# Attention stage: the first turn of the softmax weights put behind the score burst, the next tile's cast two steps later, the rotations of the opening at two places per chunk

## The chip, the cores and the metric

The kernel runs on one core of a Trainium2 chip. A core has TensorE (PE in the profile), VectorE (DVE), ScalarE (ACT), GpSimd (POOL) and SyncE (SP), each with an instruction queue of its own that is worked off in order; they meet at semaphores. DMAs are issued from the queues of SP (q1 in the profile) and ACT (q10) here. The metric is the device time of one execution in microseconds; of several executions the median counts.

## What is computed

One step of a two-layer hybrid encoder for 2048 prompt tokens and 32 sample tokens, 1024 wide. The first layer is a gated delta rule and is not touched. The second is sliding-window attention: 16 query heads of 64 elements in groups of four on 4 key heads, chunks of 64 tokens, each of which sees its own chunk and the two before it, with a learned sink in the softmax.

```
def sink_softmax(s, sinks):
    m = jnp.maximum(s.max(-1, keepdims=True), sk)
    p = jnp.exp(s - m)
    return p / (p.sum(-1, keepdims=True) + jnp.exp(sk - m))
...
def swa_layer(x, k, v, pos, cached, w_in, sinks, w_out, ln_g, ln_b):
    proj = x @ w_in
    q = rope_partial(proj[..., :B_QW].reshape(b, l, B_Q_HEADS, B_HD), pos) * (B_HD ** -0.5)
    z = proj[..., B_QW:]
    o = cached_attention(q, k, v, sk) if cached else banded_attention(q, k, v, sk)
    out = (o * jax.nn.silu(z)) @ w_out
    return layer_norm(DN_ALPHA * x + out, ln_g, ln_b)
```

## The kernel before

The program is a row of stages that are tied together by hand. Inside `with tc.manual_schedule(engines={PE, DVE, Activation})` the order of the instructions on these three engines is the order in which the Python generators emit them; the order on POOL and SP is chosen by the framework, which may put a load ahead of its place in the program. The stage that is changed is the last one: attention and output projection, from 1758 us to the end at 2180 us of the profiled execution.

Ahead of it P2 makes the projections of the second layer. Its last products (query heads for the first 416 tokens, three units of `plain`, 24 half-products of six matmuls of 128x416) are left over and are laid between the first chunks of the attention. Each half-product is one step of the generator `late`; every second step also issues a weight load on ACT's queue (L1308), and every fourth copies the finished sum from PSUM to a tile `a` on ACT (L1373) and notes down a rotation for later. `after()` takes up to two such notes: a rotation is a shuffle, two products with sin and cos and, at the following call, an addition, all on DVE (L1465 to L1472), and a store on SP (L1473). In the kernel before, `plain` calls `after()` at each step with a full product.

**One chunk** of the attention, number n, with m the one before it:

- `scores(n)`: 16 matmuls into the PSUM tile pair S (L1597), then on DVE for both halves p = 0, 1 the row maximum (L1603), the minimum with the sink (L1604) and their difference (L1605).
- `exps(n, p)`: four exponentials with row sums on ACT (L1615) and one for the sink (L1617).
- `norm(n, p)`: on DVE one over the sum (L1623, L1624), on POOL the scaling of the weights P (L1627).
- `turn(m, p)`: six transposes on PE (L1670), three into each of two PSUM tiles `tr`; the first three are copied to SBUF by ACT, the other three by DVE (both L1672). There are two `tr` buffers in all, one while the opening runs, so each of these bursts waits for the copies of the one before it.
- `values(m)`: 16 matmuls (L1695, L1700), then the product with the gate z into `graw` on DVE (L1706).

Two chunks make a tile of 128 tokens for the output projection. `ready()` takes a finished tile: it loads the residual `r` (L1784), casts `graw` to `g_hi` on ACT (L1787) and makes the remainder `g_lo` on POOL (L1788). `finish()` multiplies the tile with the output weights, 48 matmuls into `po` in eight steps of six (j = 0 to 7, lines L1818 to L1820), adds the residual (L1823) and takes the statistics of the layer norm. The norm itself is put off to step j = 2 of the following tile: an activation on ACT (L1834), a product and a sum on POOL (L1835, L1836), and the store. `outs()` strings the tiles together and calls `ready()` for the next one at the first step with j >= 4 at which one is finished.

**Order of one chunk in the loop** (`beside(n)`, 28 chunks with scores and one without):

```
scores(n); exps(n, 0); step; turn(m, 0); exps(n, 1); norm(n, 0); step; turn(m, 1); norm(n, 1); step; step; values(m)
```

A tile has eight steps and a chunk takes four, so chunks alternate: in the first of a pair (called A in what follows) the steps j = 0 to 3 run, in the second (B) j = 4 to 7, with the cast of the next tile at j = 4.

`opening()` does the same for the chunks 10 to 13 with a half-product of `late` at each `yield`; `first()` handles chunk 14, with the first four steps of the output projection.

Of the kernel before, what the change touches and what calls it, by code (L numbers as in the profile page):

```python
# [10 lines left out]
F32 = mybir.dt.float32  # L11
# [8 lines left out]
D = 1024  # L20
# [1114 lines left out]
class P2:  # L1135
# [10 lines left out]
    def __init__(self, tc, ring, right, mid, I, O, T, G):  # L1146
        self.tc, self.nc, self.I, self.O, self.T, self.G = tc, tc.nc, I, O, T, G
        self.wp = new_pool(tc, ring, "p2_w", self.RING, side="right")
        self.kp = new_pool(tc, ring, "p2_keep", 1, side="right")
        nsk = self.kp.tile([128, 8], F32, tag="nsk", name="nsk")  # L1150
        sks = self.kp.tile([128, 4], F32, tag="sks", name="sks")
        for i in range(2):
            self.nc.sync.dma_start(nsk[i * 64:i * 64 + 64, :], I["sinks"][i].partition_broadcast(64))
        for i in range(4):
            self.nc.sync.dma_start(sks[i * 32:i * 32 + 32, :], I["sinks_s"][i].partition_broadcast(32))
        for t in (nsk, sks):
            self.nc.gpsimd.tensor_scalar(out=t[:], in0=t[:], scalar1=-1.0, scalar2=None, op0=ALU.mult)
# [8 lines left out]
        self.fine = False  # L1166
        self.turn = 0
        self.todo, self.second, self.staged = [], [], []

# [170 lines left out]
        for u in units:  # L1340
            yield from (self.plain if u[2] == 0 else self.winograd)(u)

    def after(self):

        second, self.second = self.second, []
        for f in second:
            f()
        for _ in range(2):
            if self.todo:
                then = self.todo.pop(0)()  # L1350
                if then is not None:
                    self.second.append(then)

    def rest(self):
        while self.todo or self.second:
            self.after()

    def plain(self, unit):
        kind, j, _ = unit
        nc = self.nc  # L1360
        x = list(zip(*self.x0))
        for c in range(2):
            ps = (self.ppl or self.ppr).tile([128, 512], F32, tag="ps", name="ps")[:, :TB]
            for h in range(2):
                w = self.weight(unit, self.PLAIN[c][h])
                for ks in ((0, 1), (2, 3)) if self.fine else (range(4),):
                    if ks[0] == 2:
                        yield 1.13
                    self.product(ps, w, x[4 * h:4 * h + 4], h == 0, h == 1, ks)
                self.load()  # L1370
                if h == 1:
                    a = self.wk.tile([128, TB], F32, tag="ra", name="a", bufs=4)
                    nc.scalar.activation(a[:], ps, AF.Copy, scale=self.SCALES[kind])  # L1373
# [107 lines left out]
class Attention:  # L1481
# [23 lines left out]
    def open_right(self, right, pieces):  # L1505
        nc, tc = self.nc, self.tc
        R = "right"
        self.otwo = new_pool(tc, right, "u_two", 2, side=R)
        self.oone = new_pool(tc, right, "u_one", 1, side=R)
# [65 lines left out]
        return c0 * 64, nk, pair, at, one, 0 if one is None else (one - c0) * 64  # L1575

    def scores(self, n):
        nc, V, thr = self.nc, self.nc.vector, self.thr
        qs = self.start(n)[0]
        tiles = []  # L1580
        for p in range(2):
# [7 lines left out]
            else:  # L1589
# [7 lines left out]
                        nc.tensor.matmul(S[:, half, u, :nk], qs[hs, n % 2, p * 4 + 2 * u:p * 4 + 2 * u + 2, :],  # L1597
                                         kT[hs, p, k0:k0 + nk], start=True, stop=True)
                tiles.append((S[:, :, :, :nk].rearrange("r h u k -> r (h u) k"), self.nsk[:, p * 4:p * 4 + 4]))
        for p, (S, sink) in enumerate(tiles):  # L1600
            c = S.shape[1]
            nm, es_ = (thr.tile([128, 4], F32, tag=t, name=t, bufs=4) for t in ("nm", "es"))
            V.tensor_reduce(out=nm[:, :c], in_=S, axis=AX.X, op=ALU.max, negate=True)  # L1603
            V.tensor_tensor(out=nm[:, :c], in0=nm[:, :c], in1=sink, op=ALU.min)  # L1604
            V.tensor_tensor(out=es_[:, :c], in0=nm[:, :c], in1=sink, op=ALU.subtract)  # L1605
            self.probs[n, p] = S, nm, es_

    def exps(self, n, p):
        nc, thr = self.nc, self.thr
# [99 lines left out]
        elif n % 2 == 1:  # L1709
            self.pend.append(((n - 1) * 64, 128, graw))  # L1710

    def opening(self, chunks):

        yield
        yield
        for n in chunks:
            self.scores(n)
            self.exps(n, 0)
            if self.prev is None:
                self.exps(n, 1)  # L1720
                for _ in range(5):
                    yield
                self.norm(n, 0)
                self.norm(n, 1)
                yield
            else:
                for i, step in enumerate(itertools.chain(self.turn(self.prev, 0), self.turn(self.prev, 1))):
                    if i == 1:
                        self.exps(n, 1)
                    yield  # L1730
                    if i >= 2:
                        self.norm(n, i - 2)
                yield
                self.values(self.prev)
            self.prev = n
        yield

    def first(self, n):

        m, self.prev = self.prev, n  # L1740
        got = self.ready()
        self.out = self.outs(got)
        self.scores(n)
        self.exps(n, 0)
        drain(self.turn(m, 0))
        self.exps(n, 1)
        self.norm(n, 0)
        drain(self.turn(m, 1))
        self.norm(n, 1)
        for _ in range(4):  # L1750
            next(self.out)
        self.values(m)

    def beside(self, n):

        m, self.prev = self.prev, n
        if n is not None:
            self.scores(n)
            self.exps(n, 0)
        next(self.out)  # L1760
        drain(self.turn(m, 0))
        if n is not None:
            self.exps(n, 1)
            self.norm(n, 0)
        next(self.out)
        drain(self.turn(m, 1))
        if n is not None:
            self.norm(n, 1)
        next(self.out)
        next(self.out)  # L1770
        self.values(m)

    def rest(self):
# [6 lines left out]
    def ready(self):  # L1780
        nc, pool = self.nc, self.otwo
        t0, n, graw = self.pend.pop(0)
        r = pool.tile([128, D], F32, tag="r", name="r")
        nc.sync.dma_start(r[:n], self.T["h"][t0:t0 + n, :])  # L1784
        ghi = pool.tile([128, KC, 128], F32R, tag="g_hi", name="g_hi")
        glo = pool.tile([128, KC, 128], F32R, tag="g_lo", name="g_lo")
        nc.scalar.copy(ghi[:, :, :n], graw[:, :, :n])  # L1787
        nc.gpsimd.tensor_tensor(out=glo[:, :, :n], in0=graw[:, :, :n], in1=ghi[:, :, :n], op=ALU.subtract)  # L1788
        return t0, n, r, ghi, glo

    def outs(self, got):

        while got is not None:
            ahead = None
            last = self.late and not self.pend
            for j in self.finish(*got, last):
                if j == 2:
                    for f in self.todo:
                        f()
                    self.todo = []  # L1800
                if j >= 4 and ahead is None and self.pend:
                    ahead = self.ready()
                yield
            got = ahead
# [69 lines left out]
def program(tc, I, O, T, G):  # L1874
# [79 lines left out]
    with tc.manual_schedule(engines={ET.PE, ET.DVE, ET.Activation, ET.Pool}):  # L1954
# [7 lines left out]
        p2.first_keys()  # L1962
        drain(itertools.islice(late, 35))
        p2.rest()
    p2.ppl = None
    left.close()
    mid.close()
    att = Attention(tc, left, p2.keep, I, O, T, G)
    order = list(range(10, 32)) + ["s"] + list(range(10))
    p2.fine = True  # L1970
    with tc.manual_schedule(engines={ET.PE, ET.DVE, ET.Activation}):
        att.load_k(8, 14)
        att.load_v(8, 14)
        loads = iter(((14, 18), (18, 24), (24, 32)))
        for i, _ in enumerate(att.opening([order.pop(0) for _ in range(4)])):
            drain(itertools.islice(late, 1))
            if i in (8, 13, 18):
# [4 lines left out]
        p2.rest()  # L1982
        right.close()
        att.open_right(right, p2.out)
        att.first(order.pop(0))
# [147 lines left out]
```

## Time and profile before

| | us |
|---|---|
| time, median of 3 runs (2180.78 to 2184.08) | 2183.53 |
| the profiled execution's own time | 2181.37 |
| its span | 2179.6 |
| start of the scores of chunk 10 (attention begins) | 1757.97 |
| start of the scores of chunk 11, 12, 13 | 1766.58, 1787.52, 1799.69 |
| start of the scores of chunk 14 (`first`) | 1813.18 |
| start of the scores of chunk 15 (loop begins) | 1832.20 |
| end of the loop's last chunk with scores | 2137.85 |

The page gives PE 95% of the span busy, and the stretches of the table are what matters here: the opening with `first` takes 74 us, the loop 306 us, and 42 us follow. A row of the timeline gives start, duration, engine, line, operation, what it writes and reads, and in square brackets how long its engine had been idle before it and what ended that. Matmuls are pipelined, so their durations overlap; the distance between starts is the time that one costs. Rows marked ACTq or SPq are DMA issues on those queues. A row of the groups gives count, busy time and mean duration in ns, then the idle time before them and who ended it.

### The profile page before, as it was taken

Reading aid. Unit: us, or ns where it says so; the run is one execution under the profiler, and the core shown is the slowest. Engines: PE = TensorE matmul, PEld = TensorE weight load, DVE = VectorE, ACT = ScalarE, POOL = GpSimd, SP = SyncE. Lnnn points to the kernel's source line nnn. Section 1 sums busy time; section 2 is a strip of 40 time slices with the busy share of each in tenths; the row PEclk is TensorE's granted clock in tenths of the full one; section 3 lists DMA queues with packets and bytes.
Section 4 is the critical chain, followed back from the end, with each engine's and each line's share of the span. In section 5 each row is a group of like instructions: output and inputs, shape, how many; then the busy total and the mean of one; then the engine's idle time right before and its main releaser. Section 6 shows DMA issues by size and latency. Waiting matters only on the chain. (4 is left out here: it accounts for less than half of the span.)

```text
span 2179.6 us, 37384 instructions
## 1 busy us (share of the span) xinstructions
PE 2068.7 (95%) x13494; PEld 1874.1 (86%) x13494; DVE 1477.4 (68%) x2767; ACT 906.8 (42%) x2405; POOL 725.1 (33%) x1194
## 2 busy tenths in 40 slices
PE   8999999999989999999789999999999988999998
PEld 6999999999989889888778887899999976777666
DVE  5788977886557588888875665555645655666663
ACT  5545545444422476767662111411221033444441
POOL 1212211151111187878861220000000053666565
PEclk9999999999999999999999999999999999999999
DMA  7755655557764644534845675988888885433321
GB/s 283 226 187 192 214 180 185 188 180 244 257 211 157 209 128 153 163 130 152 274 144 148 209 264 192 340 290 278 291 279 282 283 291 168 110 85 93 99 81 58
DMA packets 342410, 430.28 MB, mean 197 GB/s; under 512 B 69952, under 2 KB 269984, under 8 KB 342208
## 3 DMA queue, kind: packets, MB, share of 16 engines
q1 hardware_dynamic: 304016, 304.78, 44.0%
q10 hardware_dynamic: 38208, 123.10, 16.9%
q8 instruction: 107, 1.75, 0.3%
q14 instruction: 79, 0.65, 0.1%
HBM read 269.72 MB, written 158.44 MB: 196 GB/s over the span
## 5 line engine op out<-in xcount | busy, mean ns | idle before, releaser
L77 PE MATMUL ps<-act_hi,w_hi 128*128 128x416 f32 x1280 | 458.6, 358 | 5.7 <-DVE z L322 2.5
L79 PE MATMUL ps<-act_hi,w_lo 128*128 128x416 f32 x1280 | 450.5, 353 | 4.7 <-POOL w_lo L54 3.3
L78 PE MATMUL ps<-act_lo,w_hi 128*128 128x416 f32 x1280 | 451.1, 352 | 0.0
L77 PEld LDWEIGHTS ps<-act_hi,w_hi 128*128 128x128 f32 x1280 | 242.0, 189 | 10.1 <-DVE z L322 4.3
L79 PEld LDWEIGHTS ps<-act_hi,w_lo 128*128 128x128 f32 x1280 | 241.9, 189 | 9.5 <-POOL w_lo L54 4.4
L78 PEld LDWEIGHTS ps<-act_lo,w_hi 128*128 128x128 f32 x1280 | 242.6, 190 | 2.8
L1330 PE MATMUL ps<-xs_h,w 128*128 128x416 f32 x560 | 199.6, 356 | 7.8 <-DVE ra L1391 6.6
L1331 PE MATMUL ps<-xs_l,w 128*128 128x416 f32 x560 | 199.9, 357 | 0.5 <-DVE xs_l L1228 0.5
L54 POOL TENSOR_TENSOR w_lo<-w_raw,w_hi 128x1024 fp32r<-128x1024 f32 x32 | 81.5, 2547 | 355.2 <-ACT w_hi L53 341.2
L1332 PE MATMUL ps<-xs_h,w 128*128 128x416 f32 x560 | 198.6, 355 | 0.0
L295 DVE SCALAR_TENSOR_TENSOR y<-R,convw,y 128x2083 f32<-128x2083 f32 (+2 forms) x78 | 175.1, 2245 | 24.5 <-ACT y L293 24.3
L1615 ACT ACTIVATE P<-S,nm 128x192 f32<-128x192 f32 (+2 forms) x260 | 105.3, 428 | 177.4 <-DVE nm L1604 170.8
L585 POOL TENSOR_TENSOR tm<-L,Tt 128x60 f32<-128x60 f32 (+19 forms) x375 | 136.3, 363 | 94.2 <-PE sp L760 48.9
L588 POOL TENSOR_TENSOR Tt<-Tt,tm 128x60 f32<-128x60 f32 (+19 forms) x375 | 142.0, 379 | 28.3
L1530 POOL MEMSET vd<- 64x768 f32 (+2 forms) x10 | 7.8, 776 | 398.1 <-DVE ra L1391 397.8
L1627 POOL TENSOR_TENSOR P<-P,sm 128x512 f32<-128x512 f32 (+2 forms) x126 | 101.7, 831 | 87.8 <-DVE sm L1624 69.2
L1330 PEld LDWEIGHTS ps<-xs_h,w 128*128 128x128 f32 x560 | 106.5, 190 | 10.6 <-DVE ra L1391 7.3
L1391 DVE SCALAR_TENSOR_TENSOR ra<-ps,u 128x416 f32<-128x416 f32 x60 | 35.4, 590 | 117.3 <-PE ps L1332 110.7
L1052 PE MATMUL po<-wo,g_hi 128*128 128x512 f32 (+1 forms) x272 | 110.0, 404 | 0.9 <-DVE hT L1100 0.9
L1332 PEld LDWEIGHTS ps<-xs_h,w 128*128 128x128 f32 x560 | 107.1, 191 | 1.3
L1331 PEld LDWEIGHTS ps<-xs_l,w 128*128 128x128 f32 x560 | 106.3, 190 | 2.1 <-DVE xs_l L1228 0.7
L95 ACT CAST pre_hl<-pre_raw 128x256 fp32r<-128x256 f32 x184 | 65.6, 404 | 101.4 <-DMA pre_raw<-in_b_w_z 25.8
(313 smaller groups left out, 4723.6 us busy)
## 6 DMA issues: line engine op xcount, KB each, us to landing
w<-s_w ACTq DMA_DIRECT2D x180, 512.0 KB, 4.5
s_w<-pre_hl SPq DMA_DIRECT2D x160, 256.0 KB, 2.5
w_raw<-in_w_in SPq DMA_DIRECT2D x32, 512.0 KB, 6.6
s_wo<-pre_hl SPq DMA_DIRECT2D x64, 256.0 KB, 4.1
gb<-s_gcum SPq DMA_DIRECT2D x34, 256.0 KB, 5.2
k<-s_k SPq DMA_DIRECT2D x34, 256.0 KB, 3.8
s_z<-z SPq DMA_DIRECT2D x40, 208.0 KB, 2.0
s_q<-y SPq DMA_DIRECT2D x8, 1024.0 KB, 5.2
```

The lines of the kernel that those rows point to most:

```text
L77: nc.tensor.matmul(ps, hi[:, k, :], xh[:, k, :], start=(k == 0), stop=False)
L78: nc.tensor.matmul(ps, hi[:, k, :], xl[:, k, :], start=False, stop=False)
L79: nc.tensor.matmul(ps, lo[:, k, :], xh[:, k, :], start=False, stop=(k == KC - 1))
L295: self.nc.vector.scalar_tensor_tensor(out=y[:, a:z], in0=R[:, a + j:z + j], scalar=self.convw[:, i, j:j + 1], in1=y[:, a:z], op0=ALU.mult, ...
L585: P.tensor_tensor(out=tm[:n, i0 - k:, :w], in0=L[:n, i0:, j:j + 1].to_broadcast(sh), in1=Tt[:n, j:j + 1, :w].to_broadcast(sh), op=ALU.mult)
L588: P.tensor_tensor(out=Tt[:n, i0:, :w], in0=Tt[:n, i0:, :w], in1=tm[:n, i0 - k:, :w], op=ALU.subtract)
L1052: nc.tensor.matmul(ps[:n], ghi[:, k, :n], w[0][k][:, cs], start=(k == 0), stop=False)
L1330: nc.tensor.matmul(ps, w[:, 0, k], xh[:], start=first and k == 0, stop=False, skip_group_check=True)
L1331: nc.tensor.matmul(ps, w[:, 0, k], xl[:], start=False, stop=False, skip_group_check=True)
L1332: nc.tensor.matmul(ps, w[:, 1, k], xh[:], start=False, stop=last and k == 3, skip_group_check=True)
L1615: nc.scalar.activation(P[:, u, :nk], S[:, u, :], AF.Exp, bias=nm[:, u:u + 1], scale=1.0, accum_out=sm[:, u:u + 1])
L1627: nc.gpsimd.tensor_tensor(out=out, in0=part, in1=f, op=ALU.mult)
```

## The change

Six edits, all in the last stage and in what opens it.

1. **The turn joins the burst.** `scores` no longer takes the maxima; these are a function `peaks(n, p)` of their own. `beside` is split into `head` and `tail`: after the 16 score matmuls come at once the six transposes of `turn(m, 0)`; on DVE the maxima of p = 0 stand ahead of the copy of the second three transposes, those of p = 1 behind it; on ACT the copy of the first three stands ahead of the first exponentials. Then one step of the projection, the second turn, the second exponentials and both norms, three steps, the values.
2. **The cast later.** `outs` calls `ready()` at j >= 6 in place of j >= 4, and in `ready` the load of `r` stands behind the cast.
3. **The opening** is written anew: turns, maxima and exponentials in the order of `head` and `tail`; chunk 10's norms right behind its exponentials; six half-products per chunk and no longer five.
4. **Rotations** in the opening are no longer taken up in `plain`; `after(1)` takes one note at two places of each chunk (one in chunk 10).
5. **Own buffers**: the late products' tiles `a` come from a pool of their own with three buffers (`p2_late`), where the staging tiles of P2 lay, in place of four that they shared with the earlier products.
6. `open_right` opens the pool of the output weights ahead of that of `r`, `g_hi` and `g_lo`; the loads of later keys stand at yields 8, 14, 20 in place of 8, 13, 18.

```
-            self.exps(n, 0)
             if self.prev is None:
-                self.exps(n, 1)
-                for _ in range(5):
+                for p in range(2):
+                    self.peaks(n, p)
+                    self.exps(n, p)
+                for p in range(2):
+                    self.norm(n, p)
+                for _ in range(4):
                     yield
-                self.norm(n, 0)
-                self.norm(n, 1)
+                after(1)
+                yield
                 yield
             else:
...
+                first, second = (self.turn(self.prev, p) for p in range(2))
+                next(first)
+                self.peaks(n, 0)
+                yield
+                next(first)
+                self.exps(n, 0)
+                self.peaks(n, 1)
+                yield
+                yield
+                next(second)
+                self.exps(n, 1)
+                self.norm(n, 0)
+                after(1)
+                yield
+                next(second)
+                yield
+                self.norm(n, 1)
+                after(1)
                 yield
                 self.values(self.prev)
...
     def first(self, n):
         m, self.prev = self.prev, n
+        self.out = self.outs(self.ready())
+        self.head(n, m)
+        self.tail(n, m)
+        next(self.out)
+        next(self.out)
         self.values(m)
+        next(self.out)
+        next(self.out)
+
+    def head(self, n, m):
+        turn = self.turn(m, 0)
         if n is not None:
             self.scores(n)
+        next(turn)
+        if n is not None:
+            self.peaks(n, 0)
+        next(turn)
+        if n is not None:
             self.exps(n, 0)
+            self.peaks(n, 1)
+
+    def tail(self, n, m):
+        drain(self.turn(m, 1))
         if n is not None:
             self.exps(n, 1)
             self.norm(n, 0)
+            self.norm(n, 1)
+
+    def beside(self, n):
+        m, self.prev = self.prev, n
+        self.head(n, m)
         next(self.out)
+        self.tail(n, m)
+        for _ in range(3):
+            next(self.out)
         self.values(m)
...
-                if j >= 4 and ahead is None and self.pend:
+                if j >= 6 and ahead is None and self.pend:
                     ahead = self.ready()
...
-                    a = self.wk.tile([128, TB], F32, tag="ra", name="a", bufs=4)
+                    pool, bufs = (self.late, 3) if self.late else (self.wk, 4)
+                    a = pool.tile([128, TB], F32, tag="ra", name="a", bufs=bufs)
...
-                self.after()
+                if not self.late:
+                    self.after()
```

More of the change, by code (lines that the diff above doesn't have):

```diff
@@ L1165, in __init__ @@
         self.ppl = None
-        self.fine = False
+        self.late = None
         self.turn = 0
@@ L1341, in units, with after @@
             yield from (self.plain if u[2] == 0 else self.winograd)(u)
-    def after(self):
+    def after(self, most=2):
         second, self.second = self.second, []
@@ L1347, in after @@
             f()
-        for _ in range(2):
+        for _ in range(most):
             if self.todo:
@@ L1356, in rest, with open_late @@
             self.after()
+    def open_late(self, mid):
+        self.ppl = None
+        self.late = new_pool(self.tc, mid, "p2_late", 3, side="right")
     def plain(self, unit):
@@ L1365, in plain @@
                 w = self.weight(unit, self.PLAIN[c][h])
-                for ks in ((0, 1), (2, 3)) if self.fine else (range(4),):
+                for ks in ((0, 1), (2, 3)) if self.late else (range(4),):
                     if ks[0] == 2:
@@ L1599, in scores, with peaks @@
                 tiles.append((S[:, :, :, :nk].rearrange("r h u k -> r (h u) k"), self.nsk[:, p * 4:p * 4 + 4]))
[L1600 to L1606, printed above, removed]
+        for p, t in enumerate(tiles):
+            self.probs[n, p] = t
+    def peaks(self, n, p):
+        V, thr = self.nc.vector, self.thr
+        S, sink = self.probs[n, p]
+        c = S.shape[1]
+        nm, es_ = (thr.tile([128, 4], F32, tag=t, name=t, bufs=4) for t in ("nm", "es"))
+        V.tensor_reduce(out=nm[:, :c], in_=S, axis=AX.X, op=ALU.max, negate=True)
+        V.tensor_tensor(out=nm[:, :c], in0=nm[:, :c], in1=sink, op=ALU.min)
+        V.tensor_tensor(out=es_[:, :c], in0=nm[:, :c], in1=sink, op=ALU.subtract)
+        self.probs[n, p] = S, nm, es_
     def exps(self, n, p):
@@ L1710, in values, with opening @@
             self.pend.append(((n - 1) * 64, 128, graw))
-    def opening(self, chunks):
+    def opening(self, chunks, after):
         yield
@@ L1735, in opening @@
             self.prev = n
-        yield
     def first(self, n):
         m, self.prev = self.prev, n
[L1741 to L1751, printed above, removed]
+        self.out = self.outs(self.ready())
[3 more added lines that the diff above has]
+        next(self.out)
         self.values(m)
-    def beside(self, n):
-        m, self.prev = self.prev, n
+        next(self.out)
+        next(self.out)
+    def head(self, n, m):
+        turn = self.turn(m, 0)
         if n is not None:
             self.scores(n)
+        next(turn)
[3 more added lines that the diff above has]
+        if n is not None:
             self.exps(n, 0)
-        next(self.out)
-        drain(self.turn(m, 0))
+            self.peaks(n, 1)
+    def tail(self, n, m):
+        drain(self.turn(m, 1))
         if n is not None:
@@ L1764, in beside @@
             self.norm(n, 0)
+            self.norm(n, 1)
+    def beside(self, n):
+        m, self.prev = self.prev, n
+        self.head(n, m)
         next(self.out)
[L1766 to L1770, printed above, removed]
+        self.tail(n, m)
+        for _ in range(3):
+            next(self.out)
         self.values(m)
@@ L1788, in ready @@
         nc.gpsimd.tensor_tensor(out=glo[:, :, :n], in0=graw[:, :, :n], in1=ghi[:, :, :n], op=ALU.subtract)
+        r = pool.tile([128, D], F32, tag="r", name="r")
+        nc.sync.dma_start(r[:n], self.T["h"][t0:t0 + n, :])
         return t0, n, r, ghi, glo
@@ L1974, in program @@
         loads = iter(((14, 18), (18, 24), (24, 32)))
-        for i, _ in enumerate(att.opening([order.pop(0) for _ in range(4)])):
+        for i, _ in enumerate(att.opening([order.pop(0) for _ in range(4)], p2.after)):
             drain(itertools.islice(late, 1))
-            if i in (8, 13, 18):
+            if i in (8, 14, 20):
                 a, z = next(loads)
```

16 lines of the change are left out of this document (4 added, 12 removed).

## The prediction

> **What bounds the kernel now.** Ahead of 1758 us nothing changes, so I read the last stage only: its stretches first, then the waits of PE in each.
>
> ```profile
> span 2179.6 us, 37384 instructions
> ...
> 1757.97:1813.18 55.21, 45.03 (x281) 37.98 (x280) 32.25 (x79) 19.62 (x84) 31.11 (x44) 0.91 0.86 274
> ...
> 1832.20:2137.85 305.65, 291.39 (x1867) 215.40 (x1865) 188.81 (x476) 147.22 (x583) 190.00 (x175) 1.00 0.33 87
> ```
>
> The first number behind the length is PE's busy time, the two at the end but one are the granted clock and the DMA share. In the loop PE is busy 291.39 of 305.65 us, DVE, ACT and POOL under 63%: PE bounds, and only its waits can be won. In the opening it is busy 45.03 of 55.21 at a clock of 0.91, with DMA at 0.86.
>
> ```profile
> PE tr L1670 <- ACT pt L1672: 13.2, 13, 1.4
> ...
> PE tr L1653 <- DVE pt L1656: 1.1, 1, 1.1
> ```
>
> These are all the waits of PE in the loop: 14, together 14.3 us, before transposes whose PSUM buffer had not been emptied. In opening and `first` the transposes wait too:
>
> ```profile
> L1670 PE MATMUL tr<-ident,P 128*128 128x128 f32 x48 | 9.5, 322 | 16.9 <-ACT pt L1672 11.5 <-POOL P L1627 5.3
> ```
>
> So 31.2 us of PE waits stand in the changed stretch. What causes one in the loop, from the timeline of an A chunk and the B chunk behind it:
>
> ```profile
> 1953.84 1.57 PE L1597 MATMUL S<-kT,qs 64*128 64x192 f32 x16
> 1955.35 0.50 PE L1818 MATMUL po<-w,g_hi 128*128 128x512 f32 x1
> ...
> 1956.84 0.82 PE L1670 MATMUL tr<-ident,P 128*128 128x128 f32 x6
> 1957.41 0.48 PE L1818 MATMUL po<-w,g_hi 128*128 128x512 f32 x1
> ...
> 1958.90 0.82 PE L1670 MATMUL tr<-ident,P 128*128 128x128 f32 x6
> 1959.47 0.48 PE L1818 MATMUL po<-w,g_hi 128*128 128x512 f32 x1
> ...
> 1962.43 0.65 PE L1695 MATMUL ot<-pt,vp 128*64 128x256 f32 x4
> ...
> 1964.30 1.57 PE L1597 MATMUL S<-kT,qs 64*128 64x192 f32 x16
> ...
> 1969.12 0.39 PE L1820 MATMUL po<-w,g_lo 128*128 128x512 f32 x1
> 1970.54 0.85 PE L1670 MATMUL tr<-ident,P 128*128 128x128 f32 x6 [1.02 <-ACT pt L1672]
> ...
> 1975.99 1.57 PE L1597 MATMUL S<-kT,qs 64*128 64x192 f32 x16
> ```
>
> A takes 1964.30 - 1953.84 = 10.46 us without a wait, B 11.69: the wait costs 1.23, 0.21 more than its 1.02 of idleness, as PE also drains. ACT says why:
>
> ```profile
> 1956.08 0.42 ACT L1615 ACTIVATE P<-S,nm 128x192 f32<-128x192 f32 x1 [5.75 <-DVE nm L1604]
> ...
> 1957.78 0.49 ACT L1672 COPY pt<-tr 128x384 f32<-128x384 f32 x1
> ...
> 1968.97 1.05 ACT L1787 CAST g_hi<-graw 128x1024 fp32r<-128x1024 f32 x1
> 1969.90 0.49 ACT L1672 COPY pt<-tr 128x384 f32<-128x384 f32 x1
> ```
>
> In A a half's exponentials take 1.70 (1956.08 to 1957.78) and the copy that empties `tr` follows at once. In B the cast stands between them; the copy ends at 1970.39, just before the transposes start.
>
> **The change part by part. The cast (edit 2).** Moved to j = 6 it stands on ACT behind both bursts of exponentials, when no copy is left in the chunk. So 14 waits of 14.3 us go, and 14 x 0.21 = 2.9 of draining with them: 17.2. What becomes late is `g_lo`, and what moves with it is its POOL instruction and the load of `r`.
>
> ```profile
> 1970.09 2.38 POOL L1788 TENSOR_TENSOR g_lo<-graw,g_hi 128x1024 fp32r<-128x1024 f32 x1 [2.96 <-ACT g_hi L1787]
> 1972.43 3.18 POOL L1627 TENSOR_TENSOR P<-P,sm 128x512 f32<-128x512 f32 x4
> ...
> 1971.70 0.33 SPq L1784 DMA_DIRECT2D r<-s_h  x1
> ```
>
> Counted from the start of a B chunk: the first exponentials start near 3.0 (the minimum ahead of them ends at 2.85, below) and end at 4.7, a copy takes 0.4 to the next, the second ones end at 6.8; cast 7 to 8, POOL scales P (3.18 for both halves) until 9, `g_lo` 9 to 11.4. Its first reader is the third projection matmul of the next chunk, at 10.4 + 2.1 + 0.5 = 13.0. It is covered by 1.6 us; without that cover each microsecond costs 14. `r` is first read a chunk later still (L1823); its issue on SP passes nothing that anyone waits for.
>
> **The joined turn (edit 1).** Nothing is added or removed but one passage from projection to transposes. Old, from the rows above: scores 1.51, six po 1.49, six tr 0.57, six po 1.49, six tr 0.57, twelve po 2.96, values 1.87. New: 1.51, 0.6, 1.49, 0.57, eighteen po, 1.87. Eighteen in one run instead of six and twelve saves at most 0.1; 28 chunks make 0 to 2.8, and I take 1. New waits could arise at the second turn, at 3.6 after the chunk's start (first three) and 3.9 (second three). The first three need ACT's copy, which now waits for nothing but its transposes: ready near 2.5. The second three need DVE's copy, which stands behind the maxima of p = 0:
>
> ```profile
> 1954.81 0.96 DVE L1603 TENSOR_REDUCE nm<-S 128x4 f32<-128x768 f32 x1
> ...
> 1956.08 0.95 DVE L1603 TENSOR_REDUCE nm<-S 128x4 f32<-128x768 f32 x1
> ...
> 1957.69 0.56 DVE L1672 COPY pt<-tr 128x384 f32<-128x384 f32 x1 [0.27 <-PE tr L1670]
> ```
>
> Maxima start 0.97 after the chunk and take 1.27 with their two small operations, so the copy runs 2.35 to 2.9 in A: 1.0 to spare. In B DVE is held up:
>
> ```profile
> 1966.26 0.89 DVE L1604 TENSOR_TENSOR nm<-nm,nsk 128x4 f32<-128x4 f32 x1
> ...
> 1964.76 2.38 POOL L1836 TENSOR_TENSOR r<-r,ln_b 128x1024 f32<-128x1024 f32 x1
> ```
>
> The small minimum takes 0.89 and ends with POOL's sum at 1967.14, 2.84 into the chunk. Then the copy runs about 3.2 to 3.75: 0.15 to spare. The Trainium skill (SBUF — State Buffer, Who interferes with whom) says that a VectorE instruction with two SBUF inputs and a GpSimd instruction that reads SBUF block each other for the whole instruction; by that rule this wait is fixed, and the change puts a copy behind it that PE needs. The trace agrees (0.89). I take no new wait in regular chunks. Behind the short chunks 0 to 2 POOL's sum lies later in its chunk, and I leave 0.7 of the gain there. Loop: 17.2 + 1 - 0.7 = 17.5.
>
> **The opening (edits 3 to 6).**
>
> ```profile
> 1766.58 1.57 PE L1597 MATMUL S<-kTa,qs 64*128 64x192 f32 x16
> 1773.46 0.90 PE L1670 MATMUL tr<-ident,P 128*128 128x128 f32 x3 [5.31 <-POOL P L1627]
> ...
> 1775.55 0.55 PE L1331 MATMUL ps<-x_l,w 128*128 128x416 f32 x1
> ...
> 1778.58 0.90 PE L1670 MATMUL tr<-ident,P 128*128 128x128 f32 x3 [2.14 <-ACT pt L1672]
> ...
> 1782.00 0.35 PE L1331 MATMUL ps<-x_l,w 128*128 128x416 f32 x1
> ...
> 1768.81 0.33 ACTq L1308 DMA_DIRECT2D w<-s_wo  x1
> ...
> 1775.94 0.52 ACT L1373 ACTIVATE a<-ps 128x416 f32<-128x416 f32 x1 [6.24 <-DMA w<-s_wo]
> ...
> 1778.03 0.50 ACT L1672 COPY pt<-tr 128x384 f32<-128x384 f32 x1
> ```
>
> Chunk 11's first wait ends with POOL's scaling of P, because chunk 10's norms stood on DVE behind a rotation that waited for `a`. With the norms ahead of it that wait goes. But ACT's queue is itself held: its weight loads issue at 1768.81 and later, after idle stretches that end with DMAs landing, in a stretch with DMA at 0.86, and the second `a` comes at 1775.94. In the new order the copy of the first turn stands behind this `a`, at 1776.46 to 1776.95, and with one `tr` buffer the second three transposes cannot start before. PE meanwhile has three transposes and one half-product; so it waits about as long as before (7.4 against 5.31 + 2.14), and 1.6 us earlier is all (1777.0 against 1778.58). I book 1.5. The own buffers for `a` free it from the earlier stores, but not from the loads ahead of it on its queue, so they bring nothing here. The rotation that `after(1)` puts on DVE in chunk 10 also waits for an `a` (the first follows the load of 1768.81); behind it are chunk 11's maxima, for which only ACT waits, and ACT is held longer. Edit 6 lets the last output weights load when the last half-product is done; they are read at j = 3, twelve products after the tile's start at the earliest, and I cost it at nothing (uncovered, one landing, once). Chunks 12 and 13 wait 16.9 - 5.3 - 2.1 - 6.7 = 2.8; there ACT's copy now precedes the exponentials, and these waits go, but 0.8 comes back at the end of chunk 13, where DVE's last copy stands behind a rotation and `values` behind the copy: 2.0.
>
> In `first`:
>
> ```profile
> 1814.07 1.04 ACT L1787 CAST g_hi<-graw 128x1024 fp32r<-128x1024 f32 x1
> ...
> 1815.38 2.73 DVE L1468 TENSOR_TENSOR a<-a,cos 128x416 f32<-128x416 f32 x1
> ...
> 1822.24 1.51 PE L1670 MATMUL tr<-ident,P 128*128 128x128 f32 x6 [6.68 <-ACT pt L1672]
> ```
>
> The last half-product, its copy and a whole rotation stood ahead of chunk 14's maxima, and POOL's `g_lo` stretched one product of it to 2.73. In the new order that rotation lies in chunk 13; only its addition is left. Still ACT's first copy stands behind the cast, and DVE's minimum behind `g_lo`. An estimate from the start of the scores: the cast from 1.8, when the rotation lets go of the place that `g_hi` takes over, to 2.8; `g_lo`, 2.4 as in the loop, to 5.2; minimum and copy (0.16 to 0.56 each) to 6; so the second turn's last transposes start at 6.1 where 2.4 would do: 3.7 of waiting for 6.68. With the slow clock behind the long wait (the burst took 1.51 where others take 0.85) I book 4.5. The Trainium skill (TensorE: Matmul & The Clock Gate, What's actually happening) has the clock halve after about 3.4 us of idleness; by that rule my 3.7 lies at the edge, and the sum would be 1 us smaller. The trace shows the half rate behind 5.31 (0.55 a matmul, 0.35 when over) and none behind 1.02.
>
> Opening: 1.5 + 2.0 + 4.5 = 8. Bounds: 0, where its waits only move; above, all 16.9 and the slow clock (12 half-rate matmuls x 0.2 = 2.4, and 1.5 in `first`), 20.8.
>
> **Sum.** 17.5 + 8 = 25.5. Against the profiled execution, 2181.37: 2155.9. The median of the runs shown is 2.2 higher at 2183.53, which gives 2158.0; I say 2157, between the two.
>
> **The rivals.** *ACT runs free in the opening.* If SP's loads come in another order, the weight loads wait for other DMAs; then chunk 11's 7.45 and the slow clock go as well: 2157 - 7.45 - 2.4 = 2147. For it: the framework orders SP. Against: the same loads are wanted at the same places.
>
> *DVE's copy is late in B.* The 0.15 to spare is less than I can read off; 14 chunks at up to 0.8 make 11: 2168. For it the 0.89 row, against it that POOL's sum ends early enough by the same row.
>
> *The opening gives nothing* or loses 2 by a new wait (three buffers in place of four, so that a copy waits for a store to land): 2157 + 8 to 10, 2166.
>
> *Slower: DVE becomes the bound of the joined head.* Its place is the copy behind the maxima, in every chunk and not in B alone. Its price is 28 us for each microsecond that the copy is late; it decides from 25.5 / 28 = 0.91, which means a copy 1.9 later in A than laid out. At 1.1 it makes 31 and 2183.5 - 25.5 + 31 = 2189. Against it: DVE is busy under 63% of the loop, and nothing long stands before the maxima.
>
> **How the numbers follow.** Forecast 0.50, its own range 2152 to 2163; free ACT 0.17; late copy 0.15; opening without gain 0.12; slower 0.06. Of the two middling rivals' 0.27, 0.04 lies so far out that it reaches 2179 (0.2%, 4.4 us, is about what a measurement tells from no change). That gives 0.90, 0.04, 0.06. The range 2146 to 2172 leaves out the slower case, the far ends of the middling ones and a little below.
>
> **What would show it.** Right: no PE wait before transposes in B chunks, both kinds of chunk at 10.35 to 10.46; the loop 287 to 289 us; the cast behind the second exponentials; a wait of 5 us or more in chunk 11 that ends with ACT's copy; under 4.5 in `first`. Wrong: waits of PE before the second three transposes that end with DVE, a PE wait before L1820, or chunk 11 without its long wait.

## The result, and the profile after

| | before | after |
|---|---|---|
| median, us (4 runs each) | 2182.16 | 2166.15 |
| lowest to highest | 2179.53 to 2184.08 | 2164.78 to 2170.48 |
| the profiled execution's own time | 2181.37 | 2170.48 |

The ratio is 0.9924 (95%: 0.9909 to 0.994): faster by 16 us (0.8%), where 25.5 had been forecast. The profiled execution of after is the slowest of its four. From the scores of chunk 10 to PE's last instruction it takes 400.42 us, where before took 413.43: 13.0 less, and this is what can be followed instruction by instruction (8.2 us come behind it in both, 2179.6 - 1757.97 - 413.43). The code ahead of chunk 10 does the same work in all 14 kernels of this study, and their profiles put the start of chunk 10 anywhere from 1750.37 to 1761.70. So stretches are compared below, each from one start of scores to another, and a median only where it says more than that.

The stretches of after, cut at the starts of scores as before's were: the opening, `first`, the loop.

```profile
span 2168.7 us, 37339 instructions
...
1760.10:1813.70 53.60, 45.22 (x281) 38.86 (x280) 34.05 (x79) 20.00 (x85) 31.61 (x43) 0.90 0.89 286
1813.70:1835.51 21.81, 13.51 (x69) 10.01 (x68) 8.12 (x20) 5.22 (x21) 7.10 (x7) 0.77 0.66 228
1835.51:2127.10 291.59, 290.02 (x1866) 216.25 (x1866) 198.74 (x477) 147.81 (x582) 189.49 (x175) 1.00 0.34 91
```

The loop fell from 305.65 to 291.59: 14.06 us. The opening fell by 1.6 (55.21 to 53.60), and `first` grew by 2.8 (19.02 to 21.81). PE's waits, from the chain of waits in the loop, and from the groups for opening and `first`:

```profile
PE tr L1681 <- DVE pt L1683: 0.3, 1, 0.3
...
L1681 PE MATMUL tr<-ident,P 128*128 128x128 f32 x48 | 9.3, 317 | 15.5 <-ACT pt L1683 15.5
```

Of the loop's 14.3 us, 0.3 is left in the list; the 15.5 in opening and `first` stand where 16.9 stood. An A chunk now takes 10.41, a B chunk 10.73, not 10.41 too. The B chunk that starts at 1962.04:

```profile
1962.04 1.57 PE L1603 MATMUL S<-kT,qs 64*128 64x192 f32 x16
...
1963.13 2.38 POOL L1869 TENSOR_TENSOR r<-r,ln_b 128x1024 f32<-128x1024 f32 x1
...
1964.00 1.52 DVE L1615 TENSOR_TENSOR nm<-nm,nsk 128x4 f32<-128x4 f32 x1
...
1965.64 0.55 DVE L1683 COPY pt<-tr 128x384 f32<-128x384 f32 x1
...
1966.24 0.31 PEld L1681 LDWEIGHTS tr<-ident,P 128*128 128x128 f32 x3 [0.35 <-DVE pt L1683]
...
1969.36 1.09 ACT L1818 CAST g_hi<-graw 128x1024 fp32r<-128x1024 f32 x1
```

DVE's minimum takes 1.52 and ends at 1965.52, with POOL's sum (1965.51). The copy behind it is over at 1966.19, and the second three transposes can load only then. Waits of 0.1 us are too short for the list; what they cost is seen in the length, 0.33 a chunk with the drain. The cast stands behind the second exponentials, as it was meant to.

POOL's sum ends later in its chunk than before because POOL's work starts later in the A chunk ahead of it. The first scaling of P in such a chunk, in before (scores at 1953.84) and in after (scores at 1951.63):

```profile
1958.70 1.61 POOL L1627 TENSOR_TENSOR P<-P,sm 128x512 f32<-128x512 f32 x2 [4.01 <-DVE sm L1624]
...
1957.10 1.61 POOL L1638 TENSOR_TENSOR P<-P,sm 128x512 f32<-128x512 f32 x2 [3.10 <-DVE sm L1635]
```

Chunk 11:

```profile
1768.71 1.57 PE L1603 MATMUL S<-kTa,qs 64*128 64x192 f32 x16
...
1775.66 3.17 ACTq L1308 DMA_DIRECT2D w<-s_wo  x2
...
1778.88 0.52 ACT L1378 ACTIVATE a<-ps 128x416 f32<-128x416 f32 x1 [6.99 <-DMA w<-s_wo]
1779.29 0.47 ACT L1683 COPY pt<-tr 128x384 f32<-128x384 f32 x1
...
1779.82 0.90 PE L1681 MATMUL tr<-ident,P 128*128 128x128 f32 x3 [6.47 <-ACT pt L1683]
...
1780.87 0.55 PE L1331 MATMUL ps<-x_l,w 128*128 128x416 f32 x1
...
1792.24 1.57 PE L1603 MATMUL S<-kT,qs 64*128 64x192 f32 x16
```

The copy stands behind `a`, and `a` behind two weight loads on ACT's queue. The half-products behind the wait run at 0.55 where 0.35 is full rate. Then `first`, where the time was lost:

```profile
1812.21 0.53 ACT L1378 ACTIVATE a<-ps 128x416 f32<-128x416 f32 x1
1822.82 1.04 ACT L1818 CAST g_hi<-graw 128x1024 fp32r<-128x1024 f32 x1 [10.07 <-DMA s_bq<-a]
1823.77 0.47 ACT L1683 COPY pt<-tr 128x384 f32<-128x384 f32 x1
...
1816.85 0.32 SPq L1479 DMA_DIRECT2D s_bq<-a  x1
...
1824.38 1.51 PE L1681 MATMUL tr<-ident,P 128*128 128x128 f32 x6 [8.30 <-ACT pt L1683]
```

ACT stands idle for 10.07 us until the last rotation's store, issued at 1816.85, has landed. The cast waits for it, ACT's copy for the cast, PE for the copy: 8.30 where 6.68 was. Before, the cast started at 1814.07 without a wait.

### The profile page after: what moved, and what is told of

The parts are those of the page before. It is cut to its first block, busy times and chain, and to the rows that moved or that the text cites. A ratio compares the mean times of both kernels' runs of the same rounds, so it can differ in the third digit from the quotient of the medians.

```text
span 2168.7 us, 37339 instructions
## 1 busy us (share of the span) xinstructions
PE 2071.5 (96%) x13494; PEld 1878.5 (87%) x13494; DVE 1486.6 (69%) x2767; ACT 908.2 (42%) x2405; POOL 730.5 (34%) x1194
## 3 DMA queue, kind: packets, MB, share of 16 engines
q10 hardware_dynamic: 38208, 123.10, 16.9%
## 4 chain that ended last, share of the span: by engine, by line
PE 69%; DVE 14%; DMA 5%; ACT 4%; POOL 4%; issue 3%; SPq 1%; ACTq 0%; DVEq 0%; POOLq 0%
PE ps L77 8%; PE ps L79 8%; PE ps L78 7%; PE ps L1331 5%; PE ps L1330 5%; PE ps L1332 5%; PE po L1052 3%; PE po L1054 3%; PE po L1053 3%; PE po L1851 2%; PE po L1853 2%; PE po L1852 2%; PE tr L1681 2%; PE S L1603 2%; PE ot L1706 1%
```

## The experiments

All stretches, in us, each from one start of scores to another:

| kernel | ratio to before (95%) | chunks 10 to 13 | `first` | loop, chunks 15 to 9 | from chunk 10 to PE's last |
|---|---|---|---|---|---|
| before | 1 | 55.21 | 19.02 | 295.12 | 413.43 |
| after | 0.9924 (0.9909 to 0.994) | 53.60 | 21.81 | 281.06 | 400.42 |
| 1 cast alone | 0.9948 (0.9932 to 0.9964) | 56.77 | 19.76 | 283.50 | 404.11 |
| 2 cast back | 0.9927 (0.9913 to 0.9941) | 54.29 | 21.98 | 281.34 | 401.56 |
| 3 old opening | 0.9929 (0.9913 to 0.9945) | 55.68 | 18.91 | 281.28 | 399.84 |
| 4 copy ahead of maxima | 0.9924 (0.9902 to 0.9946) | 53.53 | 21.13 | 279.14 | 398.00 |
| 5 copy ahead of minimum | 0.991 (0.9898 to 0.9923) | 53.39 | 20.70 | 276.80 | 394.86 |
| 6 old pool order | 0.9923 (0.9909 to 0.9937) | 53.69 | 18.84 | 281.24 | 397.74 |
| 7 pool for g | 0.9909 (0.9895 to 0.9923) | 54.89 | 16.17 | 283.34 | 398.08 |
| 8 fourth buffer | 0.9915 (0.9901 to 0.9928) | 55.84 | 14.19 | 281.21 | 395.18 |
| 9 tables apart | 0.9903 (0.9889 to 0.9918) | 53.94 | 15.73 | 282.85 | 396.50 |
| 10 loads on SP | 0.9921 (0.9909 to 0.9933) | 49.10 | 21.87 | 281.14 | 396.05 |
| 11 SP and fourth buffer | 0.9861 (0.9845 to 0.9878) | 43.84 | 17.71 | 281.16 | 386.65 |
| 12 all together | 0.9856 (0.9841 to 0.9871) | 43.49 | 15.69 | 277.09 | 380.25 |

Each stretch is of one execution. The opening of after's code (after, 2, 4 to 7 and 9) took 53.39 to 54.89 in chunks 10 to 13, that of before's (before, 1 and 3) 55.21 to 56.77, so differences of about 1 us there are not read.

Two theories stood at the start: that `first` lost its time to the place of `g_hi` and the loop a part of its gain to POOL's sum; and the rivals, that a queue or a lane and not the place held the cast, and that the opening's waits come from the DMAs as such.

**1. The cast alone** (before, with the step of edit 2 only; the load of `r` stays ahead of the cast).

```
-                if j >= 4 and ahead is None and self.pend:
+                if j >= 6 and ahead is None and self.pend:
```

> The kernel before with the cast at j = 6 and nothing else. By the prediction's term the 14 waits of 1.02 us before the second turn's transposes go, with 14 x 0.21 of drain: 17.2 us, 2165, ratio 0.992, and B chunks of 10.46. If the joined turn was needed for it (the copy of the first turn still stands behind exponentials that come late in B), waits of some tenths stay in B and the gain is 10 to 14 us.

Loop 283.50: 11.6 us gained. Most B chunks take 10.70 to 10.76, not 10.46. The first exponentials wait for the same minimum beside POOL's sum, and ACT's copy stands behind them, so 0.1 of idleness stays before the second turn. In three chunks a longer wait that ends with ACT's copy is left, 2.1 us in all.

**2. The cast back** (after; the load of `r` stays behind the cast).

```
-                if j >= 6 and ahead is None and self.pend:
+                if j >= 4 and ahead is None and self.pend:
```

> The changed kernel with the cast back at j = 4 (edit 2 undone). If the joined turn alone removes the 14 waits (both copies of the first turn now stand ahead of the exponentials and the cast, and the copies of the second turn have until the next chunk), this is as fast as the changed kernel, the loop within 2 us of 281.06, and the terms of edits 1 and 2 overlap. By the prediction's accounting, where the 17.2 belongs to the cast, B chunks go back to 11.4 to 11.7: 9 to 14 us slower.

Loop 281.34, as after. So either edit takes most of the 14 waits away. The joined turn alone brings 13.8, the later cast alone 11.6, and both 14.06. The last 0.3 is one chunk, number 25, which took 11.04 here with a wait of 0.42 that ends with DVE's copy; in the others the later cast brings nothing behind the joined turn.

**3. The old opening** (edits 1 and 2 on the kernel before; `opening`, `first`, `plain` and the pools are before's, with both halves' maxima right behind the scores).

```
+    def peaks(self, n, p):
...
+    def head(self, n, m):
...
+    def tail(self, n, m):
...
-                if j >= 4 and ahead is None and self.pend:
+                if j >= 6 and ahead is None and self.pend:
```

> The kernel before with the joined turn and the later cast (edits 1 and 2) and the old opening, first tile and buffers (edits 3 to 6 undone). The traces have 74.23 us from the scores of chunk 10 to those of chunk 15 before and 75.41 after, so by the theory that the new opening as a whole brought nothing this kernel is as fast as the changed one, within 2 us (2163 to 2167, ratio 0.991 to 0.993). By the prediction's term it is 8 us slower than the changed one (2174, ratio 0.996).

399.84 against 400.42, ratio 0.9929 against 0.9924: edits 3 to 6 bring nothing as a whole. Chunks 10 to 13 gain 2.1 in after, `first` loses 2.9.

**4. DVE's copy ahead of the maxima** (after; in `head`).

```
         next(turn)
-        if n is not None:
-            self.peaks(n, 0)
         next(turn)
         if n is not None:
+            self.peaks(n, 0)
             self.exps(n, 0)
```

> The changed kernel with DVE's copy of the first turn's second three ahead of the maxima in head. Theory: in B chunks the minimum of 0.17 us takes 1.52 and ends with POOL's sum, the copy behind it comes at 3.6 us after the scores and PE drains 0.33 us; with the copy ahead this goes in 13 chunks: 4.3 us, ratio to the changed kernel 0.998, all loop chunks 10.41. Rival: the exponentials start 0.6 us later, ACT's copy behind them comes late for the second turn, and in each of 28 chunks PE waits up to 0.5: slower by up to 14 us.

Half of it: 279.14. B chunks fall to 10.4, but every second A chunk rises to 10.7, and the sample chunk has a new wait of 0.52. In such an A chunk (scores at 1944.55):

```profile
1944.99 2.37 POOL L1818 TENSOR_TENSOR g_lo<-graw,g_hi 128x1024 fp32r<-128x1024 f32 x1
...
1947.42 0.50 PE L1852 MATMUL po<-w,g_lo 128*128 128x512 f32 x1
...
2010.17 0.50 PE L1852 MATMUL po<-w,g_lo 128*128 128x512 f32 x1 [0.52 <-POOL g_lo L1818]
```

The last row is the wait of the sample chunk. In the A chunk POOL is through with `g_lo` at 1947.36 and its first reader starts at 1947.42. The exponentials of B are later, with them the cast and `g_lo`: its cover, 1.15 us in after (1950.80 + 2.36 against a reader at 1954.31), is used up.

**5. The copy between maxima and minimum** (after; `peaks` takes the turn and steps it behind the reduction).

```
         V.tensor_reduce(out=nm[:, :c], in_=S, axis=AX.X, op=ALU.max, negate=True)
+        if between is not None:
+            next(between)
         V.tensor_tensor(out=nm[:, :c], in0=nm[:, :c], in1=sink, op=ALU.min)
```

> The changed kernel with DVE's copy of the first turn between the maxima and the small minimum. Theory: the minimum, which in B lasts until POOL's sum is over, no longer holds the copy, and the exponentials of B, which wait for the minimum in any case, start as before; so the 13 drains of 0.33 go, without the late g_lo that the copy ahead of the maxima brought: loop 281.06 - 4.3 = 276.8 from the scores of chunk 15 to those of chunk 9. Rival: 0.6 us later exponentials in A move something else, 0.3 a chunk: 279 or more, as with the copy first.

Loop 276.80, chunks of 10.39 and 10.41, no wait listed. The window of that loop: PE is busy through all of it.

```profile
1833.55:2110.35 276.80, 276.80 (x1798) 208.31 (x1797) 176.75 (x459) 143.44 (x561) 182.20 (x168) 1.00 0.36 95
```

**6. The old pool order** (after).

```
-        self.oone = new_pool(tc, right, "u_one", 1, side=R)
         self.otwo = new_pool(tc, right, "u_two", 2, side=R)
+        self.oone = new_pool(tc, right, "u_one", 1, side=R)
```

> The changed kernel with the two pools of open_right in their old order. Theory: in the first tile the cast to g_hi waits (10.07 us idle on ACT) because its place in u_two, behind u_one, lies on tiles whose last store lands at 1822.72. With u_two first it starts within 1 us of the scores as before, PE's wait of 8.30 falls to 4 or less, and the time falls by 5 to 8 us; but the last output weights then lie on those places, and if they land later than PE reaches j = 3, a wait of 1 to 5 us before L1851 takes some of it back. Rival: the cast waits for a lane or a queue, not for its place: the 8.30 stays and the time too.

```profile
1810.71 1.07 ACT L1818 CAST g_hi<-graw 128x1024 fp32r<-128x1024 f32 x1
...
1813.28 2.70 POOL L1819 TENSOR_TENSOR g_lo<-graw,g_hi 128x1024 fp32r<-128x1024 f32 x1
...
1814.36 2.07 DVE L1478 TENSOR_TENSOR a<-a,rs 128x416 f32<-128x416 f32 x1
...
1818.21 0.55 PE L1681 MATMUL tr<-ident,P 128*128 128x128 f32 x3 [3.13 <-DVE pt L1683]
...
1827.46 0.50 PE L1852 MATMUL po<-wo,g_hi 128*128 128x512 f32 x1 [0.64 <-DMA wo<-s_wo]
```

The cast comes 1.1 us ahead of the scores (1811.80). What is left is the chain of the prediction, `g_lo` that stretches DVE's addition to 2.07 and DVE's copy behind it: 0.39 and 3.13 of waiting where 3.7 had been estimated. Three waits for weights (0.64, 0.53, 0.77) take 1.9 back, as expected. `first` gains 3.0 and not 5 to 8; the rival, by which the 8.30 stays, is out.

**7. A pool for `g`** (after; `g_hi`, `g_lo` lowest, then the weights, `r` last).

```
+        self.og = new_pool(tc, right, "u_g", 2, side=R)
         self.oone = new_pool(tc, right, "u_one", 1, side=R)
         self.otwo = new_pool(tc, right, "u_two", 2, side=R)
```

> The changed kernel with g_hi and g_lo in a pool of their own at the bottom of the right side, where x0 lay, the output weights above it and r and the small tiles last, over the late products. Theory: neither the cast nor the weights then wait for the last stores, only the load of r does; the first tile has the 3.5 of wait that the old pool order showed and not its 1.94 before L1852, so it takes 17 us instead of 21.81. Rival: the weights land late because of the DMAs ahead of them and not because of the stores: 18.9 as with the old order.

`first` falls to 16.17, without a wait for weights; but chunk 15 takes 12.93 where 10.39 stood, so 3.1 of the 5.6 us stay.

```profile
1813.66 1.19 SPq L1822 DMA_DIRECT2D r<-s_h  x2
...
1824.67 0.69 DVE L1857 SCALAR_TENSOR_TENSOR r<-r,po 128x512 f32<-128x512 f32 x1 [5.44 <-PE tr L1682]
...
1825.41 0.50 PE L1852 MATMUL po<-w,g_hi 128*128 128x512 f32 x1 [1.60 <-DVE r L1857]
```

The load of `r` goes out behind the weights and tables on SP. The residual that reads it holds DVE until 1824.67; the releaser in the bracket is PE, but its transposes were long done. PE waits 1.60 for the bank that the residual empties. That it is the load that DVE waits for is inferred from the order.

**8. A fourth late buffer** (after).

```
-        self.late = new_pool(self.tc, mid, "p2_late", 3, side="right")
+        self.late = new_pool(self.tc, mid, "p2_late", 4, side="right")
...
-                    pool, bufs = (self.late, 3) if self.late else (self.wk, 4)
+                    pool, bufs = (self.late, 4) if self.late else (self.wk, 4)
```

> The changed kernel with four late buffers in place of three and the weight loads still on ACT: splits what four buffers and SP did together. Theory: in the changed kernel the copies of the opening stand behind weight loads and not behind a buffer, so the fourth buffer alone does nothing there: chunks 10 to 13 at 53 to 55 us, as with three, and only with the loads on SP, when the copies come early enough to meet the stores, does it count. Rival (the prediction's): three buffers in place of four held the changed kernel, and four alone bring the 53.60 to 50 or less.

Chunks 10 to 13 gain nothing, as expected; 55.84 is even a little over the 53 to 55. What was not expected is `first`, 14.19, the shortest of all:

```profile
1814.58 1.05 ACT L1818 CAST g_hi<-graw 128x1024 fp32r<-128x1024 f32 x1 [4.22 <-DVE a L1478]
...
1816.15 0.85 PE L1681 MATMUL tr<-ident,P 128*128 128x128 f32 x6 [2.46 <-ACT pt L1683]
...
1818.12 0.50 PE L1853 MATMUL po<-w,g_lo 128*128 128x512 f32 x1 [0.65 <-POOL g_lo L1819]
```

The cast waits for DVE's last addition and for no store. This is the chain that the prediction laid out for `first`: the cast 3.3 after the scores, 3.11 of waiting where 3.7 had been estimated, and 4.8 us less than before where 4.5 had been booked. The pool order (6), a pool of its own (7) and a fourth buffer (8) each free the cast from the last store, so it is a matter of place. No view shows which tile lay under `g_hi`.

**9. Tables apart, both copies on ACT** (after; old pool order, `ln_g` and `ln_b` in a third pool above the weights, and in `first` ACT makes both copies of the first turn).

```
+        otab = new_pool(tc, right, "u_tab", 1, side=R)
...
+        for copy in (nc.scalar.copy, nc.scalar.copy if both else V.tensor_copy):
```

> The changed kernel with u_two first again, the tables ln_g and ln_b in a pool of their own above the output weights, so that only they lie on the late products, and with both copies of the first turn in the first tile on ACT. Theory: the old order left 3.13 us of wait that ends with DVE's copy behind its addition (2.07 us beside POOL's g_lo) and 1.94 us for weights whose loads waited for the last store; ACT is idle there, so its copy frees the transposes about 3 us earlier, and the weights start 2.4 us earlier: first tile 15 to 16.5 us instead of 21.81, chunk 15 at 10.4. Rival: the weights land when the DMAs get to them, and PE waits for them by as much as it comes earlier: 18 to 19.

`first` 15.73: the 3.13 is gone. The weights still land late (1.51, 0.61, 0.74 of waiting; 2.9 in place of 1.9), so PE came earlier than they did, and this half of the rival holds. Chunk 15 takes 12.04 and not 10.4, with a granted clock of 0.86, so 1.6 of the gain is lost again behind `first`.

**10. The weight loads on SP** (after; in `load`).

```
-                    self.nc.scalar.dma_start(flat.bitcast(F32), self.T["wo"][1][slot // 2, :, slot % 2])
+                    self.nc.sync.dma_start(flat.bitcast(F32), self.T["wo"][1][slot // 2, :, slot % 2])
```

> The changed kernel with the loads of the output weights during the opening issued by SP instead of ACT. Theory: in chunk 11 ACT's copy of the turn stands behind two of these loads, whose issues at 1775.66 and 1778.50 come right behind landings at 1775.56 and 1778.43; with them on SP the copy follows its transposes, the wait of 6.47 goes, and with it half-rate matmuls of some 2 us: 4 to 9 us faster than the changed kernel in the stretch from the scores of chunk 10 to those of chunk 15. Rival: the stretch is held by the DMAs themselves (share 0.89), so that PE waits for a landing in another place, or SP's key and value loads fall behind the weight loads: no gain, or some us lost.

Chunk 11 falls from 23.53 to 11.68, without any wait. Chunk 12 rises from 11.69 to 19.05:

```profile
1787.50 0.22 ACT L1628 ACTIVATE es<-es 128x4 f32<-128x4 f32 x1
1793.61 0.52 ACT L1378 ACTIVATE a<-ps 128x416 f32<-128x416 f32 x1 [5.89 <-DMA s_bq<-a]
...
1794.55 0.55 PE L1681 MATMUL tr<-ident,P 128*128 128x128 f32 x3 [3.85 <-ACT pt L1683]
```

With three buffers `a` waits for the landing of an earlier store. A wait of 1.71 that ends with POOL's scaling of P stands ahead of it in the same chunk. So 4.5 of 11.9 us stay as a gain.

**11. SP and a fourth buffer** (after, with the edits of 8 and 10).

> The changed kernel with the weight loads of the opening on SP and four late buffers in place of three. With the loads on SP alone, the 6.47 in chunk 11 went and 3.85 came in chunk 12, behind an a that had waited for the landing of an earlier store (5.89). Theory: a fourth buffer takes this wait away: chunks 10 to 13 in 45 to 47 us instead of 49.10 and 53.60. Rival: the copy then waits for the fourth store or for a landing in another place, and 49 stays.

43.84, better than expected, with one wait left in chunk 12 and the full clock:

```profile
1783.72 0.55 PE L1681 MATMUL tr<-ident,P 128*128 128x128 f32 x3 [2.04 <-POOL P L1638]
...
1759.83:1803.67 43.84, 41.80 (x281) 36.48 (x281) 33.27 (x79) 19.99 (x85) 30.73 (x43) 1.00 1.05 330
```

The opening was not held by the DMAs as such: for the same 281 matmul rows they move 330 GB/s here and 286 in after. The two edits count for more together than apart: 9.8 us in these chunks, where the loads on SP alone bring 4.5 and the fourth buffer alone nothing. `first`, 17.71, is not as short as in (8): the cast starts 5.0 after the scores, and the page does not settle what held it.

**12. All together** (after, with the edits of 5, 8, 9 and 10).

> The changed kernel with all that the runs point to: DVE's copy between maxima and minimum, weight loads on SP and four late buffers, the pools of the first tile so that neither the cast nor the weights wait for the last stores, both copies of its first turn on ACT. From the scores of chunk 10 to the end 400.42 in the changed kernel; less 4.3 (loop), 4.5 to 8 (opening) and 5 to 6.5 (first tile): 382 to 387, ratio to before 0.986, about 2152. Rival: the first tile's weights come no earlier and the opening's waits only move: 390.

380.25, better than expected and the shortest of these stretches; median 2152.87 (4 runs), 1.4% faster than before. Its B chunks show why 5 works:

```profile
1841.91 2.39 POOL L1872 TENSOR_TENSOR r<-r,ln_b 128x1024 f32<-128x1024 f32 x1
...
1843.04 0.56 DVE L1686 COPY pt<-tr 128x384 f32<-128x384 f32 x1 [0.49 <-PE tr L1684]
1843.51 0.81 DVE L1618 TENSOR_TENSOR nm<-nm,nsk 128x4 f32<-128x4 f32 x1
```

The copy takes 0.56 beside POOL's sum, the minimum behind it 0.81 until the sum is over. `first` with chunk 15 takes 26.1 (15.69 and 10.40): less than in (11), 28.1, and more than with the fourth buffer alone (8), 24.6.

## Why the prediction was right, and where its sum was wrong

Faster was right, and so was the bound: PE's waits, of which the loop's list keeps 0.3 us. The time was 9 us too low: it lies outside the forecast's own range of 2152 to 2163, and inside 2146 to 2172 only because that covers the rivals too. Of the 25.5, the loop brought 14.06 for 17.5, the opening's chunks 1.6 for 3.5, and `first` -2.8 for 4.5.

- **The cast.** That the 14 waits go was right, and that they cost 17.2 nearly so: with the minimum out of the way (5) the loop gains 18.3, where the prediction's terms make 17.5. But the whole term was put to one edit, where either takes most of it: 11.6 for the cast alone (1), 13.8 for the joined turn alone (2). The joined turn sets both copies of the first turn ahead of the exponentials and the cast, which by itself frees the second turn. The prediction counted for it only the passage that it saves.
- **"0.15 to spare in B", no new wait taken.** This step failed. POOL's sum starts 1.09 after the scores (1963.13 - 1962.04), where it started 0.46 after them before, since the scalings ahead of it on POOL start 0.6 later in the A chunk (5.47 after its scores for 4.86, the rows above). The minimum ends 3.48 into the chunk and not 2.84, and the copy is over at 4.15. Eleven B chunks pay 0.33 or a little more and chunk 2 pays 0.55: 4.3, which (5) gives back (281.06 - 276.80). The rival with this mechanism had the right place and a price of 11. Beside POOL's sum the minimum, with two inputs in SBUF, took 1.52 and 0.81 where it takes 0.16 or 0.17 in the A chunks, and the copy out of PSUM took its usual 0.56. The Trainium skill (SBUF — State Buffer, Who interferes with whom) has it so: a VectorE instruction with two SBUF inputs contends with a GpSimd instruction that reads SBUF, and one with at most one such input, outside the two-port modes, does not. The trace agrees (0.81 and 0.56).
- **`g_lo` covered by 1.6.** It was 1.15, and (4) shows the price once the cover is gone.
- **Chunk 11.** The wait of 5 us or more that ends with ACT's copy was there (6.47), and its cause is shown by (10). The gain of 1.5 did not come: the copy was over 11.05 after the scores, where the prediction had it at 10.37, and waits of 1.19 and 0.72 came beside it. That the own buffers "bring nothing here" was right for the fourth one alone (8) and wrong once the loads are off ACT (11).
- **`first`.** The step that failed is "the cast from 1.8, when the rotation lets go of the place that `g_hi` takes over". It came at 9.1 (1822.82 - 1813.70), because not the rotation but the store behind it lets go. Edit 6, costed at nothing but for a late landing of weights, put the pool there, and three buffers in place of four (edit 5) let the last store lie under it. With the fourth buffer the rotation does let go of the cast, and the estimate holds (8): 3.11 of waiting for 3.7, 4.8 gained for 4.5. The 3.5 in (6) come near it partly by luck, as the cast stood ahead of the scores there.
- **The rivals.** "The opening gives nothing", or loses 2 because a copy waits for a store to land, was given 0.12 and 2166. That is what came in the opening, with the cast in the place of the copy, and the late copy in B beside it. That the median is 2166 too is luck: by the traces the opening fell short by 9.2 and the loop by 3.4, together 12.6, where the forecast and the median differ by 9. "ACT runs free in the opening" needs the loads on another queue and a fourth buffer; the kernel that has both (11) took 2155.35, not 2147.
- **The signs.** Of those named for right, the cast behind the second exponentials and the long wait in chunk 11 came. B chunks of 10.73, a loop of 291.59 (287 to 289 was named) and a wait of 8.30 in `first` did not fit, and a sign of being wrong came: the second three transposes held by DVE's copy.

## What to carry to other kernels

When a pool is moved onto another's place, ask what its first writer will wait for. Here it was the landing of a store and not its issue (issued at 1816.85, the cast at 1822.82); look for the last DMA out of the old tiles and ask whose queue the new writer would block. Two edits that cure the same wait are not to be added: ask of each what it does alone. A wait that leaves one engine's queue can come back at the next scarce thing (here a buffer), so price the pair and not the single edit.

## What the runs showed of the hardware

In (9) the half rate came behind short waits:

```profile
1821.96 0.50 PE L1853 MATMUL po<-wo,g_hi 128*128 128x512 f32 x1 [1.51 <-DMA wo<-s_wo]
...
1825.21 2.88 PE L1604 MATMUL S<-kT,qs 64*128 64x192 f32 x16
```

With 1.51, 0.61 and 0.74 us of idleness in four microseconds the next scores took 2.88 and not 1.57, and the chunk 12.04 at a granted clock of 0.86. In (12), with 0.12, 0.78, 0.55 and 1.09 before the same weights, the next chunk took 10.40 at 1.00. The Trainium skill (TensorE: Matmul & The Clock Gate, What's actually happening) has the clock halve after an idle window of about 3.4 us. Here 2.9 us in pieces came ahead of the half rate once and 2.5 did not. Nor is it the sum alone: in (8) waits of 2.46 and 0.65 within four and a half microseconds left the clock at 1.00. No run here shows what decides. The work ahead of chunk 10, the same in all kernels, differed by 11 us between profiles, at granted clocks (means of the whole execution) of 0.983 at the latest start and 0.990 at the earliest.
